# A two-layer trunk on one core: tokens loaded by halves, transposes moved ahead of a last pass, a weight split moved behind the turned h, an add moved to GpSimd

## The chip, the cores and the metric

The kernel runs on one core of one Trainium2 chip. The metric is the device time of one launch in microseconds (us). Engines are named as in the profile: PE (TensorE, matmuls) with PEld (its weight loads), DVE (VectorE), ACT (ScalarE), POOL (GpSimd), SP (SyncE, which here only issues DMAs).

## The reference

Two layers over 256 tokens of width 1024, all in float32. Each layer has a SwiGLU FFN (inner width 2816), a mixer of parallel head groups (SSD, pooling, attention) and a second FFN, each between two RMSNorms:

```python
for l in range(DEPTH):                      # DEPTH = 2
    f = swiglu(rmsnorm(h, ff1_norm_pre[l]), ff1_w_gate[l], ff1_w_up[l], ff1_w_down[l])
    h = h + 0.5 * rmsnorm(f, ff1_norm_post[l])
    m = hybrid_mixer(rmsnorm(h, mix_norm_pre[l]), w_in[l], ..., w_out[l])
    h = h + rmsnorm(m, mix_norm_post[l])
    f = swiglu(rmsnorm(h, ff2_norm_pre[l]), ff2_w_gate[l], ff2_w_up[l], ff2_w_down[l])
    h = h + 0.5 * rmsnorm(f, ff2_norm_post[l])
```

where `swiglu(x, wg, wu, wd) = (silu(x @ wg) * (x @ wu)) @ wd`.

## The kernel before, in words

*Precision.* Every float32 operand of a matmul is cut into two parts, hi (rounded to fp32r) and lo = raw − hi, and a product is hi·hi + lo·hi + hi·lo, three matmuls. For a weight, ACT writes hi (L103) and DVE lo (L104). For activations the same is done by `split_into` (L209 on ACT, L210 on DVE).

*Weights.* The class `Weights` streams all weights in the order of use as units of 1 MB: four slots for raw units (loaded by SP, L78) and five for split ones. `pump` loads the next unit when a slot is free, and otherwise issues the next split. A job can first add a second unit to the first (L102, on DVE). So the time when a unit's load goes out depends on when the work on the unit before it in that slot is finished.

*Tokens.* Two tiles of 128 tokens. Before a sub-layer, `pre_scale` normalises a tile: two squares with sums on ACT (`square_sum`, L226), the sum with eps (L215 on DVE, L218 on ACT), a power −0.5 on POOL (L220), and the scaling on DVE (L252). `pre_turn` then transposes it on PE (L261) and splits the result into xT. For an FFN it also builds the sums and differences of tile quarters that a quad needs (S1 to S4). `post` does the norm behind a sub-layer and adds to h (L234, L243). A tile's work stands beside the other tile's matmuls.

*FFN.* The inner width has 11 blocks of 256. Blocks 0 and 1 come first (`ffn_first`, once per token tile; its matmuls are in `mm_half`, L324). Blocks 4, 7 and 10 are pairs (L305). The others are computed two at a time as quads (`ffn_quad`), by a Strassen-like scheme of seven products (`product`, L435) with the factors X11·g1, S1·T1, S2·T2, S3·T3, X12·g2, X22·T4 and S4·u2. T1 = g1 + u1, T2 = g1 + u2 and T4 = g1 + g2 are formed in the raw buffer of g1; T3 is formed by POOL's accumulating load (L108), which adds u2 to u1 in place. Between the products stand the down matmuls of earlier blocks (`mm_rows`, L341), whose moving operand is the transposed h (`turn`: four PE transposes per half at L410, then the splits into t).

*Mixer.* `first(t)` computes q, k, v of a tile: L313 (`mm_tok`) and L324 (`mm_half`), then the tile's rotary terms.

*Order.* A tile framework takes the instructions in program order and lets its scheduler move those that no `keep_in_program_order` or `issue_after` holds. At the start, SP loads raw0 in one piece, then raw1 in two, x's second tile and the next units; ACT's queue loads x's first tile (L165) and the gains. Constants are loaded after the first quad's `later()`.

Of the kernel before, what the change touches and what calls it, by code (L numbers as in the profile page):

```python
# [14 lines left out]
ALU = mybir.AluOpType  # L15
# [32 lines left out]
class Weights:  # L48
# [23 lines left out]
    def load(self, pieces=1):  # L72
        i = self.loaded
        src, cols = self.units[i]
        t = self.rawp.tile([P, KD * QDT], F32, tag="raw", name=f"raw{i}")
        step = cols // pieces
        for c in range(0, cols, step):
            self.nc.sync.dma_start(t[:, c : c + step], src[:, c : c + step])  # L78
        self.raw[i] = t
        self.loaded += 1  # L80
        self.live += 1
# [32 lines left out]

    def pump(self):
        while True:
            if self.loaded < len(self.units) and self.live < RAW_BUFS:
                self.load()
            elif self.split < len(self.jobs) and self.held < SPLIT_BUFS and self.ready():
                self.split_next()  # L120
            else:
                return
# [16 lines left out]
def hybrid_trunk_kernel(ctx: ExitStack, tc: tile.TileContext, a, out: bass.AP):  # L139
# [24 lines left out]
    h = consts.tile([P, NT, D], F32, name="h")  # L164
    nc.scalar.dma_start(h[:, 0, :], a["x"][:P, :])  # L165
    grow = [buf(tag="n"), buf(tag="n")]
# [45 lines left out]
    def rsqrt_sum(ssq, eps):  # L212

        v, r = tiny(1), tiny(1)
        nc.vector.tensor_scalar(v, ssq[0], eps, None, op0=ALU.add)  # L215
        for s in ssq[1:]:
            w = tiny(1)
            nc.scalar.activation(w, s, AF.Identity, bias=v)  # L218
            v = w
        nc.gpsimd.tensor_tensor(r, v, halfexp, op=ALU.pow)  # L220
        return r

    def square_sum(x, n, gain=1.0):
# [5 lines left out]
    def post(t, f, gain, store=None):  # L229

        fg = [buf(tag="n"), buf(tag="n")]

        def scaled(i):
            nc.vector.tensor_tensor(fg[i], f[i], gains[:, 1, i * 512 : (i + 1) * 512], op=ALU.mult)  # L234

        ssq = [square_sum(f[0], D, gain)]
        scaled(0)
        ssq.append(square_sum(f[1], D, gain))
        r = rsqrt_sum(ssq, EPS / (gain * gain))
        scaled(1)  # L240
# [14 lines left out]
    def pre_turn(t, xn, left=None, late=False):  # L255
# [40 lines left out]
        for i, (name, k, t_) in enumerate((("X11", 0, 0), ("X12", 4, 0), ("X22", 4, 1))):  # L296
# [17 lines left out]

    def mm_half(ps, us, t, pin=False):
# [29 lines left out]
    def plan_ffn(l, n):  # L345
# [15 lines left out]
        for i in range(2, NU):  # L361
# [5 lines left out]
            elif i in QUADS:  # L367
                src = a[f"ff{n}_q"][l, QUADS.index(i)]
                g1, u1, u2 = (W.unit(src[k]) for k in (0, 1, 3))
                p["g1", i] = W.job(g1)  # L370
                p["T1", i] = W.job(g1, (g1, ALU.add, u1), then=(u1, src[3]))
# [24 lines left out]

    def ffn_first(t, p, pin=False):

        ps = [bank(), bank()]
        for i in range(2):  # L400
            mm_half(ps[i], [p["f", i, k] for k in range(2)], t, pin)
        hf = gate(*ps)
        W.pump()
        return hf
# [34 lines left out]
    def ffn_quad(i, p, left, turn, downs):  # L439
# [12 lines left out]
        turn(1)  # L452
        W.pump()
        if "rest" in left:
            left.pop("rest")()
        pb = bank()
# [28 lines left out]
    def ffn(l, n, p, gain, turned, left, next_left, before_next, last, later=None):  # L485

        acc = [None, None]
        hT = {}
        hf = [ffn_first(0, p, pin=later is not None)]
        turned()  # L490
        hf.append(ffn_first(1, p))

# [13 lines left out]
        for i in range(2, NU):  # L506
# [18 lines left out]
            if later:  # L525
                later()
# [10 lines left out]
        if last:  # L537
            post(1, acc[1], gain, before_next)
            return None
        post(1, acc[1], gain)  # L540
        xn1 = before_next(1)
        W.pump()
        return lambda: pre_turn(1, xn1, left=next_left)


    def plan_mix(l):
# [3 lines left out]
        for i, k in enumerate(("B", "C", "x0", "x1", "u")):  # L550
            p[k] = W.plan(a["w_in"][l, i], pieces=2 if i else 4)
        for k in range(2):
# [4 lines left out]

    def mixer(l, p, turned, next_left, before_next):
# [3 lines left out]
        nc.sync.dma_start(row, a["row"][l : l + 1, :].to_broadcast([P, R_ALL]))  # L562

        qk, v, dtr = [], [], small.tile([P, NT, HEADS], F32, tag="dtr", name=f"dtr{l}", bufs=1)

        def first(t):
# [4 lines left out]
            mm_half(pkv, [p["kv", k] for k in range(2)], t)  # L571
            c = buf()
            nc.scalar.activation(c[:, :256], pq[:, :256], AF.Copy)
            nc.vector.tensor_tensor(dtr[:, t, :], pq[:, 256:QDT], row[:, R_DTB : R_DTB + HEADS], op=ALU.add)
            nc.scalar.activation(c[:, 256:], pkv[:, :256], AF.Copy)
            w = buf(n=256)
# [14 lines left out]

        first(0)
        turned()
        first(1)
# [335 lines left out]
        W.done(p["ws1"])  # L930
        post(1, acc[1], 1.0)
        xn1 = before_next(1)
        W.pump()
        return lambda: pre_turn(1, xn1, left=next_left)
# [155 lines left out]
```

## Time and profile before

| | us |
|---|---|
| median of 3 runs | 946.64 (946.31 to 946.86) |
| profiled execution, its own time | 946.24 |
| its span | 944.5 |
| PE busy | 927.3 (98%) |
| PEld busy | 792.5 (84%) |
| DVE busy | 789.1 (84%) |
| ACT busy | 580.8 (61%) |
| POOL busy | 34.9 (4%) |
| DMA | 190.56 MB, mean 202 GB/s |

The clock that PE was granted is full (1.00) in the whole span but its end. The profile is of one execution; the time of that execution is 1.7 us longer than its span. A row of the timeline gives the start, the length, the instruction (out<-in, partitions x elements) and how often it stands in a row; in brackets stands how long the engine idled before it and what released it.

### The profile page before, as it was taken

The numbers are of one execution on the slowest core, as the hardware profiler recorded it, in microseconds if no ns is written. First come the engines' busy times: TensorE is split into PE (matmuls) and PEld (weight loads), VectorE is DVE, ScalarE is ACT, GpSimd is POOL, SyncE is SP. The second block draws the span as 40 slices with busy tenths as digits, with TensorE's granted clock in tenths as the row PEclk, the third lists the DMA queues.
The fourth block names the chain that finished last, engine by engine and source line by source line (L and its number), as shares of the span: only waits on it lengthen the run. The fifth ranks groups of instructions, "written<-read, shape, count | busy, mean of one in ns | idle before, by whom it ended". The sixth has DMA issues, their size and how long they took to land.

```text
span 944.5 us, 13133 instructions
## 1 busy us (share of the span) xinstructions
PE 927.3 (98%) x5058; PEld 792.5 (84%) x5058; DVE 789.1 (84%) x1067; ACT 580.8 (61%) x923; POOL 34.9 (4%) x47
## 2 busy tenths in 40 slices
PE   7999999999999999999999999999999999999997
PEld 4779898989888789898887888898898887989895
DVE  5899898589887998989499989876888799989872
ACT  5666656468737575747467656556694566656651
POOL 1000000010001000000010000000000010000000
PEclk9999999999999999999999999999999999999999
DMA  8757767555343476758463958583833263858531
GB/s 318 224 216 264 263 182 279 213 190 212 134 149 136 135 272 210 284 148 297 173 196 116 352 143 307 146 318 117 275 128 134 90 201 122 329 180 281 177 116 45
DMA packets 28004, 190.56 MB, mean 202 GB/s; under 512 B 3107, under 2 KB 3363, under 8 KB 5925
## 3 DMA queue, kind: packets, MB, share of 16 engines
q1 hardware_dynamic: 25920, 176.34, 51.0%
q0 software_dynamic: 1728, 12.58, 7.3%
q8 instruction: 40, 0.66, 0.3%
q10 hardware_dynamic: 292, 0.79, 0.2%
q14 instruction: 24, 0.19, 0.1%
HBM read 188.65 MB, written 1.05 MB: 201 GB/s over the span
## 4 chain that ended last, share of the span: by engine, by line
PE 85%; DVE 6%; ACT 5%; issue 2%; DMA 2%; POOL 0%; DVEq 0%; POOLq 0%; ACTq 0%
PE acc L341 26%; PE wk L435 22%; PE wk L305 21%; PE wk L324 10%; DVE lo L104 3%; ACT hi L103 3%; PE wk L410 1%; ACT n L226 1%; DMA raw<-in_ff_q 1%; DVE raw L102 1%; PE wk L873 1%; PE wk L261 1%; DMA n<-in_gains 1%; ACT xT L209 1%; POOL s L220 0%
## 5 line engine op out<-in xcount | busy, mean ns | idle before, releaser
L104 DVE TENSOR_TENSOR lo<-raw,hi 128x1024 fp32r<-128x1024 f32 (+2 forms) x440 | 468.1, 1101 | 58.5 <-ACT hi L103 57.5
L103 ACT ACTIVATE hi<-raw 128x1024 fp32r<-128x1024 f32 (+2 forms) x440 | 400.0, 959 | 167.3 <-DVE raw L102 45.4
L341 PE MATMUL acc<-hi,t 128*128 128x512 f32 x832 | 219.9, 394 | 1.8 <-ACT t L209 1.3
L341 PEld LDWEIGHTS acc<-hi,t 128*128 128x128 f32 x832 | 153.1, 188 | 36.4 <-ACT t L209 5.0
L305 PE MATMUL wk<-xT,hi 128*128 128x256 f32 x1088 | 143.5, 284 | 0.0
L305 PEld LDWEIGHTS wk<-xT,hi 128*128 128x128 f32 x1088 | 136.6, 191 | 1.6
L341 PE MATMUL acc<-lo,t 128*128 128x512 f32 x416 | 114.5, 390 | 0.0
L435 PE MATMUL wk<-hi,n 128*128 128x512 f32 x384 | 102.6, 390 | 1.2 <-DVE t L210 1.2
L324 PE MATMUL wk<-hi,xT 128*128 128x512 f32 x384 | 101.1, 396 | 1.8 <-ACT xT L209 1.0
L341 PEld LDWEIGHTS acc<-lo,t 128*128 128x128 f32 x416 | 78.1, 188 | 16.5
L102 DVE TENSOR_TENSOR raw<-raw,raw 128x1024 f32<-128x1024 f32 x72 | 86.1, 1216 | 3.4 <-DMA raw<-in_ff_q 3.4
L324 PEld LDWEIGHTS wk<-hi,xT 128*128 128x128 f32 x384 | 71.1, 189 | 18.9 <-ACT hi L103 2.2
L435 PEld LDWEIGHTS wk<-hi,n 128*128 128x128 f32 x384 | 71.8, 188 | 17.2 <-issue 2.4
L435 PE MATMUL wk<-hi,xT 128*128 128x512 f32 x288 | 77.8, 392 | 0.0
L305 PE MATMUL wk<-xT,lo 128*128 128x256 f32 x544 | 76.8, 283 | 0.0
L305 PEld LDWEIGHTS wk<-xT,lo 128*128 128x128 f32 x544 | 70.3, 192 | 0.0
L435 PEld LDWEIGHTS wk<-hi,xT 128*128 128x128 f32 x288 | 53.6, 188 | 11.5 <-DVE t L466 0.7
L209 ACT ACTIVATE t<-wk 128x256 fp32r<-128x256 f32 x72 | 26.8, 375 | 43.3 <-DVE t L210 22.1
L324 PE MATMUL wk<-lo,xT 128*128 128x512 f32 x192 | 52.6, 393 | 0.1
L435 PE MATMUL wk<-lo,n 128*128 128x512 f32 x192 | 51.5, 389 | 0.0
L234 DVE TENSOR_TENSOR n<-acc,gains 128x512 f32<-128x512 f32 x24 | 16.5, 687 | 35.8 <-ACT n L226 35.8
L324 PEld LDWEIGHTS wk<-lo,xT 128*128 128x128 f32 x192 | 35.9, 188 | 8.6 <-DVE lo L104 1.0
(172 smaller groups left out, 764.8 us busy)
## 6 DMA issues: line engine op xcount, KB each, us to landing
raw<-in_ff_q SPq DMA_DIRECT2D x48, 1024.0 KB, 5.0
raw<-in_ff_d SPq DMA_DIRECT2D x44, 1024.0 KB, 5.0
raw<-in_ff_f SPq DMA_DIRECT2D x16, 1024.0 KB, 6.0
raw<-in_ff_q POOLq DMA_DIRECT2D x12, 1024.0 KB, 8.0
raw<-in_ff_g SPq DMA_DIRECT2D x12, 1024.0 KB, 4.8
raw<-in_ff_u SPq DMA_DIRECT2D x12, 1024.0 KB, 4.9
raw<-in_w_in SPq DMA_DIRECT2D x10, 1024.0 KB, 4.9
raw<-in_w_kvz SPq DMA_DIRECT2D x8, 1024.0 KB, 5.2
```

Of the source, the lines that this page charges most:

```text
L102: nc.vector.tensor_tensor(raw[:, s], self.raw[x][:, s], self.raw[y][:, s], op=op)
L103: self.act = nc.scalar.activation(hi[:, s], raw[:, s], AF.Copy)
L104: nc.vector.tensor_tensor(lo[:, s], raw[:, s], hi[:, s].bitcast(F32), op=ALU.subtract)
L209: split_into.last = nc.scalar.activation(hi, src_f32, AF.Copy)
L226: nc.scalar.activation(junk, x, AF.Square, scale=1.0 / (gain * math.sqrt(n)), accum_out=ssq)
L234: nc.vector.tensor_tensor(fg[i], f[i], gains[:, 1, i * 512 : (i + 1) * 512], op=ALU.mult)
L261: nc.tensor.transpose(ps[:, k * P : (k + 1) * P], xn[i][:, k * P : (k + 1) * P], ident)
L305: nc.tensor.matmul(ps, w[:, k, s], y[:, k, :], start=i == 0 and k == 0, stop=i == 2 and k == KD - 1)
L324: m = nc.tensor.matmul(ps, y[:, k, :], w[:, k, :], start=h == 0 and n == 0, stop=h == 1 and n == len(parts) - 1)
L341: nc.tensor.matmul(acc[b], x[:, j, s], w[:, j, b * 512 : (b + 1) * 512], start=first and j == 0 and i == 0, stop=last and j == 1 and i == 2)
L410: nc.tensor.transpose(ps[:, k * P : (k + 1) * P], hf[:, k * P : (k + 1) * P], ident)
L435: nc.tensor.matmul(ps, x[:, k, :], w[:, k, :], start=first and n == 0, stop=n == len(parts) - 1, skip_group_check=not first)
```

## The change

1. x's first tile is loaded in two halves: the left on SP, ahead of raw0, the right on ACT's queue. raw0 is loaded in two pieces, and two of its four pieces are split ahead of the first xT.
2. `mm_half` takes a function `ahead`, which it calls before the last four matmuls of its second half: the second tile's transposes stand there (in `ffn_first` of the first tile, in the mixer's `first(0)`).
3. In `ffn_quad` the second tile's factors for S3 and S4, and the splits that `pump` issues there (the third factor T3 first), are issued behind the turned h. Those for S1 and S2 (`middle`) move into the second `ffn_first`. The first quad's g1 is split in four pieces instead of two.
4. The eps add moves from DVE to GpSimd (28 instructions); `post` computes both squares ahead of its scalings.
5. Constants, gains, and the first mixer's parameters are loaded behind a later unit, and cast when that unit's split is done; `pump` holds fewer units at some calls, and runs behind a named instruction at others.

The core of the diff:

```diff
@@ def pump
-    def pump(self):
+    def pump(self, most=SPLIT_BUFS):
...
-            elif self.split < len(self.jobs) and self.held < SPLIT_BUFS and self.ready():
+            elif self.split < len(self.jobs) and self.held < most and self.ready():
...
-    nc.scalar.dma_start(h[:, 0, :], a["x"][:P, :])
+    nc.sync.dma_start(h[:, 0, :512], a["x"][:P, :512])
+    nc.scalar.dma_start(h[:, 0, 512:], a["x"][:P, 512:])
...
@@ def rsqrt_sum
-        nc.vector.tensor_scalar(v, ssq[0], eps, None, op0=ALU.add)
+        nc.gpsimd.tensor_scalar(v, ssq[0], eps, None, op0=ALU.add)
...
+    def pump_behind(ins):
+        with tc.issue_after(ins.ins):
+            W.pump()
...
@@ def post
-        ssq = [square_sum(f[0], D, gain)]
+        ssq = [square_sum(f[i], D, gain) for i in range(2)]
+        r = rsqrt_sum(ssq, EPS / (gain * gain))
         scaled(0)
-        ssq.append(square_sum(f[1], D, gain))
-        r = rsqrt_sum(ssq, EPS / (gain * gain))
         scaled(1)
...
@@ def pre_turn
+        def middle():
+            part("S1", s1)
+            nc.vector.tensor_tensor(x11, s1, x11, op=ALU.subtract)
+            part("S2", x11)
...
-        part("S1", s1)
         nc.vector.tensor_tensor(s3, x11, turned[0], op=ALU.subtract)
-        nc.vector.tensor_tensor(x11, s1, x11, op=ALU.subtract)
-        part("S2", x11)
-        left["rest"] = rest
+        left["middle"], left["rest"] = middle, rest
...
@@ def mm_half
+                if ahead and h == 1 and n == 8:
+                    ahead()
...
@@ def ffn_first
-        W.pump()
+        if between:
+            W.split_next()
+            between()
+
+        W.pump(SPLIT_BUFS - t)
...
@@ def ffn_quad
         turn(1)
-        W.pump()
         if "rest" in left:
-            left.pop("rest")()
+            with tc.issue_after(split_into.last.ins):
+                left.pop("rest")()
+                W.pump()
+        else:
+            W.pump()
...
@@ def ffn
-        hf = [ffn_first(0, p, pin=later is not None)]
-        turned()
-        hf.append(ffn_first(1, p))
+        hf = [ffn_first(0, p, later is not None, turned)]
+        middle = left.pop("middle")
+        if later is None:
+            middle()
+        hf.append(ffn_first(1, p, between=middle if later else None))
...
@@ def mixer
-        first(0)
-        turned()
+        first(0, turned)
         first(1)
...
-    W.load()
+    W.load(2)
...
-    W.split_next((0,))
+    W.split_next((0, 1))
...
     def later():
-        more_constants()
-        load_gain(1, 0, 1)
-        load_gain(0, 0, 2)
+        with tc.issue_after(W.dma.ins):
+            more_constants()
+            load_gain(1, 0, 1)
+            load_gain(0, 0, 2)
+            params[0] = load_params(0)
+        with tc.issue_after(W.act.ins):
+            cast_constants()
```

How the instructions stand, before and now, at three places. (Line numbers shift with the change: L209 becomes L214, L210 L215, L324 L336, L261 L269.) First ACT in the first quad of the first FFN. hi6 is the right factor T2, hi7 a down unit, hi8 the factor T3 that the accumulating load completes; t45 and t47 are the turned h. Before:

```order
L103 ACTIVATE hi5_358<-raw4_198 128x1024
L103 ACTIVATE hi6_367<-raw4_198 128x1024
L103 ACTIVATE hi7_375<-raw7_214 128x1024 x2
L209 ACTIVATE t45_391<-wk49_395 128x2x128
L103 ACTIVATE hi8_383<-raw5_200 128x1024
L103 ACTIVATE hi6_367<-raw4_198 128x1024
L103 ACTIVATE hi8_383<-raw5_200 128x1024
L209 ACTIVATE t45_391<-wk54_434 128x2x128
L209 ACTIVATE t47_393<-wk49_395 128x2x128
L209 ACTIVATE t47_393<-wk54_434 128x2x128
```

Now:

```order
L103 ACTIVATE hi6_373<-raw4_200 128x1024
L103 ACTIVATE hi7_381<-raw7_216 128x1024
L214 ACTIVATE t45_389<-wk49_393 128x2x128
L214 ACTIVATE t47_391<-wk49_393 128x2x128
L463 ACTIVATE t51_415<-wk50_402 128x512
L467 ACTIVATE t53_430<-wk52_417 128x512
L214 ACTIVATE t45_389<-wk54_432 128x2x128
L214 ACTIVATE t47_391<-wk54_432 128x2x128
L214 ACTIVATE n55_441<-t34_289 128x512
L103 ACTIVATE hi8_450<-raw5_202 128x1024
```

The splits of hi8 stood between the halves of t45; they now stand behind both t45 and t47, and behind n55, the split of one of the left factors.

Second, PE at the start of the first layer's mixer. The rows L324 (now L336) are `mm_half` of the first tile, with hi43 and hi44 the weights of k and v; L261 (now L269) are the second tile's transposes. Before:

```order
L313 MATMUL wk154_1796<-hi42_1567,xT1_104 128x264 x8
L324 MATMUL wk155_1797<-hi43_1747,xT0_103 128x512 x4
L324 MATMUL wk155_1797<-lo43_1748,xT0_103 128x512 x4
L324 MATMUL wk155_1797<-hi43_1747,xT1_104 128x512 x4
L324 MATMUL wk155_1797<-hi44_1759,xT0_103 128x512 x4
L324 MATMUL wk155_1797<-lo44_1760,xT0_103 128x512 x4
L324 MATMUL wk155_1797<-hi44_1759,xT1_104 128x512 x4
L261 MATMUL wk159_1859<-ident_82,n152_1741 128x128 x4
```

Now:

```order
L323 MATMUL wk154_1794<-hi42_1577,xT1_105 128x264 x8
L336 MATMUL wk155_1795<-hi43_1757,xT0_104 128x512 x4
L336 MATMUL wk155_1795<-lo43_1758,xT0_104 128x512 x4
L336 MATMUL wk155_1795<-hi43_1757,xT1_105 128x512 x4
L336 MATMUL wk155_1795<-hi44_1769,xT0_104 128x512 x4
L336 MATMUL wk155_1795<-lo44_1770,xT0_104 128x512 x4
L269 MATMUL wk157_1843<-ident_83,n152_1751 128x128 x4
L269 MATMUL wk158_1850<-ident_83,n153_1752 128x128 x4
```

The transposes stood behind all 24 matmuls; they now stand ahead of the last four.

Third, DVE in the first quad of the second FFN. raw51 holds g1, and the sum L102 adds g2 from raw55 to it for T4; lo64 belongs to T3, lo65 to g2, and lo66 to the next down unit. Before:

```order
L104 TENSOR_TENSOR lo64_3065<-raw52_2871,hi64_3064 128x1024 x2
L210 TENSOR_TENSOR t331_3073<-wk334_3076,t330_3072 128x2x128
L210 TENSOR_TENSOR t331_3073<-wk339_3115,t330_3072 128x2x128
L286 TENSOR_TENSOR t295_2811<-t295_2811,t294_2809 128x512
L210 TENSOR_TENSOR t333_3075<-wk334_3076,t332_3074 128x2x128
L210 TENSOR_TENSOR t333_3075<-wk339_3115,t332_3074 128x2x128
L102 TENSOR_TENSOR raw51_2617<-raw51_2617,raw55_3062 128x1024
L210 TENSOR_TENSOR n343_3144<-t295_2811,n342_3143 128x512
L104 TENSOR_TENSOR lo65_3125<-raw55_3062,hi65_3124 128x1024 x2
L458 TENSOR_TENSOR t336_3098<-wk344_3147,t336_3098 128x512
L104 TENSOR_TENSOR lo66_3131<-raw56_3070,hi66_3130 128x1024 x2
```

Now:

```order
L215 TENSOR_TENSOR n341_3131<-t319_2978,n340_3130 128x512
L102 TENSOR_TENSOR raw51_2627<-raw51_2627,raw55_3076 128x1024
L215 TENSOR_TENSOR n343_3136<-t295_2821,n342_3135 128x512
L104 TENSOR_TENSOR lo64_3140<-raw52_2881,hi64_3139 128x1024 x2
L104 TENSOR_TENSOR lo65_3148<-raw55_3076,hi65_3147 128x1024 x2
L477 TENSOR_TENSOR t336_3104<-wk344_3161,t336_3104 128x512
L102 TENSOR_TENSOR raw51_2627<-raw51_2627,raw55_3076 128x1024
L478 TENSOR_TENSOR wk337_3106<-wk337_3106,t336_3104 128x512
L484 TENSOR_TENSOR wk349_3224<-wk349_3224,t336_3104 128x512
L485 TENSOR_TENSOR t338_3119<-t338_3119,wk349_3224 128x512
L104 TENSOR_TENSOR lo66_3154<-raw56_3145,hi66_3153 128x1024 x2
```

The T4 sum's first half stood behind lo64, and lo66 one row behind L458, the sum with T2's product. Now that half of the T4 sum and one split of a left factor stand ahead of lo64, and between L477 (the former L458) and lo66 stand four more: the T4 sum's second half, the difference with T2's product (L478), and the two with T3's product (L484, L485).

## Rows read from the trace of the kernel before

**Rows 1.** The page: busy time of PE; groups, with idle time and releaser.
```profile
PE 927.3 (98%) x5058; PEld 792.5 (84%) x5058; DVE 789.1 (84%) x1067; ACT 580.8 (61%) x923; POOL 34.9 (4%) x47
...
L341 PE MATMUL acc<-hi,t 128*128 128x512 f32 x832 | 219.9, 394 | 1.8 <-ACT t L209 1.3
...
L435 PE MATMUL wk<-hi,n 128*128 128x512 f32 x384 | 102.6, 390 | 1.2 <-DVE t L210 1.2
L324 PE MATMUL wk<-hi,xT 128*128 128x512 f32 x384 | 101.1, 396 | 1.8 <-ACT xT L209 1.0
```

**Rows 2.** Chain of waits, first us 50 to 75: start, length, what.
```profile
56.69 5.44 PE wk L435 x24
```

**Rows 3.** Windows from 13 to 180 us: length, busy time by engine, clock, DMA.
```profile
13.00:40.00 27.00, 25.57 (x111) 19.15 (x110) 25.00 (x36) 22.20 (x41) 1.91 (x2) 1.00 0.76 266
40.00:50.00 10.00, 8.72 (x41) 6.88 (x40) 7.00 (x7) 5.14 (x7) 0.00 (x0) 1.00 0.75 198
50.00:180.00 130.00, 129.46 (x717) 112.71 (x716) 115.31 (x126) 81.74 (x103) 1.75 (x2) 1.00 0.71 243
```

**Rows 4.** Timeline of the start: start, length, instruction, idle before and its releaser.
```profile
0.79 0.41 ACTq L165 DMA_DIRECT2D h<-in_x  x1
...
7.30 0.63 ACT L226 ACTIVATE n<-h 128x512 bf16<-128x512 f32 x1 [3.73 <-DMA h<-in_x]
...
7.64 3.75 PE L945 MATMUL acc<-n,n 128*128 128x512 f32 x4 [2.57 <-DMA n<-in_gains]
...
13.88 3.75 ACT L103 ACTIVATE hi<-raw 128x512 fp32r<-128x512 f32 x7
...
28.51 1.20 PE L324 MATMUL wk<-hi,xT 128*128 128x512 f32 x4 [0.23 <-ACT xT L209]
```

**Rows 5.** DMA of the first 25 us, 40 slices.
```profile
GB/s 0 0 39 131 184 446 406 413 465 387 469 423 433 406 367 433 472 419 419 433 420 433 419 380 0 0 0 0 223 170 419 419 419 420 419 433 433 341 406 419
```

**Rows 6.** Timeline, 37 to 54 us, around the turned h.
```profile
37.25 1.03 POOL L108 DMA_DIRECT2D raw<-in_ff_q  x1 [13.70 <-DVE raw L102]
...
45.94 2.95 ACT L103 ACTIVATE hi<-raw 128x1024 fp32r<-128x1024 f32 x3 [4.02 <-DMA raw<-in_ff_q]
...
49.21 0.98 PE L341 MATMUL acc<-hi,t 128*128 128x512 f32 x3 [1.27 <-ACT t L209]
...
51.86 1.88 PE L341 MATMUL acc<-hi,t 128*128 128x512 f32 x7 [0.52 <-DVE t L210]
```

**Rows 7.** Timeline, first layer's mixer start, 199 to 212 us.
```profile
199.36 1.06 ACT L103 ACTIVATE hi<-raw 128x1024 fp32r<-128x1024 f32 x1
...
205.38 1.41 DVE L252 SCALAR_TENSOR_TENSOR n<-h,s,gains 128x512 f32<-128x512 f32 x2 [0.44 <-POOL s L220]
...
208.21 1.25 PE L313 MATMUL wk<-hi,xT 128*128 128x264 f32 x8 [0.36 <-ACT xT L209]
...
211.19 0.55 PEld L313 LDWEIGHTS wk<-hi,xT 128*128 128x128 f32 x4 [0.32 <-DVE xT L210]
```

**Rows 8.** Line L220, whole span, and one instance from the timeline.
```profile
L220 POOL TENSOR_TENSOR s<-s,halfexp x28: 547/870/1437, 9.5 to 939.5; 128x1 f32<-128x1 f32 x28
...
304.25 1.44 POOL L220 TENSOR_TENSOR s<-s,halfexp 128x1 f32<-128x1 f32 x1 [3.42 <-ACT s L218]
```

**Rows 9.** Timeline, 326 to 343 us, first quad of the second FFN.
```profile
326.59 0.33 SPq L78 DMA_DIRECT2D raw<-in_ff_q  x1
...
331.38 1.23 DVE L102 TENSOR_TENSOR raw<-raw,raw 128x1024 f32<-128x1024 f32 x1 [0.63 <-DMA raw<-in_ff_q]
...
336.00 2.35 DVE L104 TENSOR_TENSOR lo<-raw,hi 128x1024 fp32r<-128x1024 f32 x2
...
338.27 0.70 DVE L459 TENSOR_TENSOR wk<-wk,t 128x512 f32<-128x512 f32 x1
...
342.69 1.07 PE L341 MATMUL acc<-lo,t 128*128 128x512 f32 x4
```

**Rows 10.** Timeline, ACT at 110 us.
```profile
109.99 2.01 ACT L103 ACTIVATE hi<-raw 128x1024 fp32r<-128x1024 f32 x2 [2.48 <-issue]
```

More of the change, by code (lines that the diff above doesn't have):

```diff
@@ L77, in load @@
         for c in range(0, cols, step):
-            self.nc.sync.dma_start(t[:, c : c + step], src[:, c : c + step])
+            self.dma = self.nc.sync.dma_start(t[:, c : c + step], src[:, c : c + step])
         self.raw[i] = t
@@ L194, in more_constants, with cast_constants @@
         nc.sync.dma_start(cst, a["consts"])
+    def cast_constants():
         nc.scalar.activation(after_r, after, AF.Copy)
@@ L214, in rsqrt_sum @@
         v, r = tiny(1), tiny(1)
-        nc.vector.tensor_scalar(v, ssq[0], eps, None, op0=ALU.add)
+        nc.gpsimd.tensor_scalar(v, ssq[0], eps, None, op0=ALU.add)
         for s in ssq[1:]:
             w = tiny(1)
-            nc.scalar.activation(w, s, AF.Identity, bias=v)
+            rsqrt_sum.last = nc.scalar.activation(w, s, AF.Identity, bias=v)
             v = w
@@ L313, in mm_tok, with mm_half @@
                 nc.tensor.matmul(ps, x[:, k, s], w[:, k, :], start=i == 0 and k == 0, stop=i == 2 and k == KD - 1)
-    def mm_half(ps, us, t, pin=False):
+    def mm_half(ps, us, t, pin=False, ahead=None):
         for h, u in enumerate(us):
@@ L369, in plan_ffn @@
                 g1, u1, u2 = (W.unit(src[k]) for k in (0, 1, 3))
-                p["g1", i] = W.job(g1)
+                p["g1", i] = W.job(g1, pieces=2 if i > QUADS[0] else 4)
                 p["T1", i] = W.job(g1, (g1, ALU.add, u1), then=(u1, src[3]))
@@ L395, in gate, with ffn_first @@
         return hf
-    def ffn_first(t, p, pin=False):
+    def ffn_first(t, p, pin=False, ahead=None, between=None):
         ps = [bank(), bank()]
         for i in range(2):
-            mm_half(ps[i], [p["f", i, k] for k in range(2)], t, pin)
+            mm_half(ps[i], [p["f", i, k] for k in range(2)], t, pin, ahead if i else None)
         hf = gate(*ps)
-        W.pump()
+        if between:
+            W.split_next()
+            between()
+        W.pump(SPLIT_BUFS - t)
         return hf
@@ L524, in ffn @@
                 before = [i, i + 1]
-            if later:
+            if later and i in PAIRS:
                 later()
@@ L540, in ffn, with turn_second @@
         post(1, acc[1], gain)
+        summed = rsqrt_sum.last
         xn1 = before_next(1)
-        W.pump()
-        return lambda: pre_turn(1, xn1, left=next_left)
+        W.pump(SPLIT_BUFS - 1)
+        def turn_second():
+            pre_turn(1, xn1, left=next_left)
+            pump_behind(split_into.last)
+        if next_left is not None:
+            pump_behind(summed)
+            return lambda: pre_turn(1, xn1, left=next_left)
+        return turn_second
     def plan_mix(l):
@@ L550, in plan_mix @@
         for i, k in enumerate(("B", "C", "x0", "x1", "u")):
-            p[k] = W.plan(a["w_in"][l, i], pieces=2 if i else 4)
+            p[k] = W.plan(a["w_in"][l, i], pieces=2 if i > 1 else 4)
         for k in range(2):
@@ L556, in plan_mix, with load_params @@
         return p
-    def mixer(l, p, turned, next_left, before_next):
+    params = {}
+    def load_params(l):
         vec = small.tile([P, V_ALL], F32, tag="vec", name=f"vec{l}", bufs=1)
@@ L562, in mixer, with first @@
         nc.sync.dma_start(row, a["row"][l : l + 1, :].to_broadcast([P, R_ALL]))
+        return vec, row
+    def mixer(l, p, turned, next_left, before_next):
+        vec, row = params.pop(l) if l in params else load_params(l)
         qk, v, dtr = [], [], small.tile([P, NT, HEADS], F32, tag="dtr", name=f"dtr{l}", bufs=1)
-        def first(t):
+        def first(t, ahead=None):
             pq, pkv = bank(), bank()
@@ L570, in first @@
             last and W.done(p["q"])
-            mm_half(pkv, [p["kv", k] for k in range(2)], t)
             c = buf()
@@ L574, in first @@
             nc.vector.tensor_tensor(dtr[:, t, :], pq[:, 256:QDT], row[:, R_DTB : R_DTB + HEADS], op=ALU.add)
+            mm_half(pkv, [p["kv", k] for k in range(2)], t, ahead=ahead)
             nc.scalar.activation(c[:, 256:], pkv[:, :256], AF.Copy)
@@ L931, in mixer @@
         post(1, acc[1], 1.0)
+        summed = rsqrt_sum.last
         xn1 = before_next(1)
-        W.pump()
+        W.pump(SPLIT_BUFS - 1)
+        pump_behind(summed)
         return lambda: pre_turn(1, xn1, left=next_left)
@@ L947, in hybrid_trunk_kernel @@
     left = {}
-    W.split_next((0,))
+    W.split_next((0, 1))
     keep = pre_turn(0, xn0, left=left, late=True)
     with tc.issue_after(split_into.last.ins):
-        W.split_next((1, 2, 3))
+        W.split_next((2, 3))
         W.load()
```

## The prediction

> **What bounds the kernel now.** I read the head of the page first: PE is busy in 98% of the span [rows 1]. So only what keeps PE from starting, or makes it stop, can change the time. Then the chain of waits: it consists of stretches of matmuls at a fixed pace, 24 of them in 5.44 us (0.227 us each) [rows 2]. The change leaves the number of matmuls as it is, so a gain has to be a PE stall. The groups of the page with their idle time, and then the timeline around each, list the stalls that the diff touches: the start of the program, the wait on the turned h (1.3 of the 1.8 us of the first group shown), the wait on xT (1.0) and three waits on t before a quad's first product (1.2) [rows 1]. Last, the busy time by stretch tells who has room: DVE has 2.0 us left of 27 (13 to 40 us) and 3.0 of 10 (40 to 50), and 14.7 of 130 after that [rows 3]. The reader is to see that PE is first, but DVE only a few us behind it.
>
> **A. The start.** Before, x's first tile (512 KB, one load on ACT's queue, out at 0.79) travels beside raw0's 1 MB. The first square starts at 7.30 after 3.73 us of waiting for x, the matmul that spreads the gains at 7.64 for the gains' row, and the first matmul of the second token tile, behind all the work on the first, at 28.51 [rows 4]. The row of GB/s has slices of 0.625 us: its first ten sum to 1.54 MB at 6.25 us [rows 5], so x arrived with all of raw0, and was seen 1.05 us after that. Now one half of x goes ahead of raw0 on SP, the other on ACT's queue. By the same row 0.50 MB have moved at 3.75 us and 0.75 MB at 4.4. If x shares with nothing, it is seen at 4.8, if the second half shares with raw0, at 5.4. The square of the last half then starts at 4.8 to 5.4 instead of 7.93 (7.30 and one square of 0.63): 2.5 to 3.1 us earlier. The gains' row, queued behind one half, must come as much earlier; I allow 0.3 for it and take −2.4. Further, ACT had one half-unit split ahead of xT and seven behind it (3.75 us, 0.54 each) [rows 4]; it now has two ahead, in time in which it waits anyway, and six behind: −0.54. Sum −2.94, taken as −3.0. Bounds: −1.0 (x seen only 0.5 earlier, and the piece) and −3.5.
> The Trainium skill ("DMA: Bandwidth & Descriptors", Rules for kernel authors) says that two transfers to two halves of the partitions, or spread over issuing engines, share the same 16 DMA engines and bring no bandwidth. The trace agrees as far as it goes: 406 to 469 GB/s while both queues ran, and 419 later with SP's alone [rows 5]. By that rule alone the split would bring nothing, and the sum would be 942.9 (rival 2); but what I count is how many bytes stand ahead of x, not bandwidth.
>
> **B. The turned h in the first quad.** Before, on ACT, the splits of hi8, the third right factor, stand between the two halves of the turned h. They need the unit that POOL's accumulating load completes: out at 37.25, and ACT stands idle for 4.02 us until 45.94. PE therefore waits 1.27 us at 49.21 for ACT's t, and 0.52 at 51.86 for DVE's [rows 6]. Behind each the first matmuls are slow (three in 0.98 where the pace gives 0.68), so together they cost some 2.0 to 2.1. Now the turned h stands ahead of hi8, so both go: −2.0. What is late next: hi8 itself. With A the accumulate goes out near 33 and, if it takes the same 8.6 us, lands near 41.5; PE has the second product and 24 down matmuls (2.7 and 5.4 us) between the turned h and hi8, so hi8 has cover for about 8 us from 42 on. If the cover were gone, its two splits (2 us) would be the price. DVE must follow: A and B take 5.0 us out of a stretch in which it has 2.0 and 3.0 idle [rows 3]. It just fits; each lo that slips costs its slip. Bounds of B: 0 and −2.2.
>
> **C. The mixer's start, twice.** Before, the transposes of the second tile wait at the end of a chain: two squares on ACT with a 1024-wide hi (1.06) between them and the sum, pow on POOL, h, two more squares, DVE's eps add, pow, the scaling (205.38), transposes, xT; PE waits 0.36 for ACT at 208.21 and the weight load 0.32 for DVE at 211.19 [rows 7]; with the slower matmuls behind, some 0.8. Now the two 1024-wide splits are behind, so the sum starts near 199.5, and the scaling near 204.5; and the transposes are emitted ahead of the last four of 24 matmuls, so that xT's split lies beside those (0.9 us). Either would do: I take −0.6 for each of two layers, −1.2, and leave 0.2 each for what the new order costs. Bounds: +0.3 (two adds on POOL of 0.55 each in the chain, against the 0.8) and −0.85 each. The eps add (28 instructions) goes from DVE to POOL. A 128x1 POOL operation lasts 0.55 at the shortest, 0.87 in the median, and 1.44 at 304.25, beside a DVE subtraction [rows 8]. On the paths here it stands behind the first square, and the second square (0.63) still runs beside it, so nothing; without that cover 0.55 to 1.4 a piece, in the chains of C.
> The Trainium skill ("SBUF — State Buffer", Who interferes with whom) goes against this edit: a DVE instruction with two SBUF inputs holds the read port that GpSimd needs. The long pow beside a lo agrees [rows 8]. By it the add could wait one lo, and C would shrink to 0.2 a layer: 941.2, which stays within the forecast's own range.
>
> **D. The first quads of the three later FFNs.** Before, PE waits 1.2 us for t in all ahead of three first products [rows 1], 0.4 each. Now the second product (2.7 us) stands ahead of the down matmuls, and the transposes ahead of the last matmuls of `ffn_first`: that wait, the like for xT at the FFN's start (1.0 in all with the 0.23 of the program's start [rows 1, 4]), and the slow matmuls behind both could go, up to 1.2 in each. But DVE, which works in order, now has the sum for T4 (L102) in front of the splits of the third factor, and that sum waits for the unit of g2: out at 326.59, when the unit before it is cut, seen at 331.38 (4.8 us) [rows 9]. From there to the first lo half of the next down weights DVE has: that sum 1.23, one 0.69, four lo at 1.18, one 0.70, a second sum 1.23, three at 0.70 and the lo 1.18: 11.8 by busy times, 11.0 if each starts 0.07 before the last one's end as in the trace. That is 342.4 to 343.2; PE used this lo at 342.69. So DVE takes back what PE gains: 0. Bounds −1.2 and +1.7 each (the second if the next unit, whose slot comes free only with the third factor's last lo, lands late too).
>
> **E. At nothing.** Constants, gains, vec and row are loaded behind the 20th unit (near 100), and their casts come a few us later: they lie beside ACT idle time such as the 2.48 at 109.99 [rows 10]; without it 2 us. In post both squares come first, which matters in C alone. The tail: the last sum waits for the second square as before, so the add hides. Units cut in four pieces instead of two cost ACT under 0.1 a pair (two of 0.54 against one of 1.06), beside its third of idle time after 50 us [rows 3].
>
> **Sum.** The profiled execution took 946.24, the median of the runs is 946.64, 0.4 above it. 946.24 − 3.0 − 2.0 − 1.2 = 940.0; with the 0.4 the forecast is 940.4 us.
>
> **Rivals.**
> 1. *The first quads gain in full*: the unit of g2 lands sooner, or DVE is not the one PE waits for. For it: PE's stalls there are real [rows 1]; against: DVE's 11.8 us. 940.4 − 3 × 1.2 = 936.8.
> 2. *Tokens no earlier*: the halves still arrive with raw0, since the same DMA engines serve both; A is 0.5. 946.64 − 0.5 − 2.0 − 1.2 = 942.9. Against it: the first 0.5 MB is there by 3.75 us.
> 3. *DVE gives the lead back*: with its room of 5.0 us used up, half of A and B returns as waits for lo before 55 us. 940.4 + 2.5 = 942.9; with C lost too, 944.1, or 944.7 with D at +0.2 each.
> 4. *Slower*: DVE's T4 sum waits for g2. Place: the first quad of three FFNs, on DVE, with every lo of the quad queued behind it and PE waiting for those. If g2 takes 8.6 us to land, as the accumulate did [rows 6], instead of 4.8, the lo is there at 346.2 where PE wants it at 342.69: 3.5 each, 10.5 in all, 950.9. It decides (slower by 0.2% than before) from 2.7 us each, which is a landing of some 7.8 us. For it: the order on DVE is certain; against it: the same kind of load took 4.8 with the same queue.
>
> **Chances.** Forecast 0.50 (own range 938.0 to 942.3), rival 1 0.14, rival 2 0.14, rival 3 0.13, rival 4 0.09. A measurement of this kernel can tell 0.2% (1.9 us) from no change: faster means under 944.7. Forecast, rivals 1 and 2 and half of 3 are faster, 0.84; the other half of 3 (C lost too, and more) is within 0.2%, 0.07; rival 4 is slower, 0.09. The range 936.5 to 945.0 takes in 1 to 3.
>
> **What would show it.** A: the first square near 5 us and tile 1's first matmul near 25.5; if the square is at 6.5 or later, rival 2. B: no PE idle above 0.3 between the first products, and hi8 in place before PE asks for it. C: PE's gap at the L313 matmuls of tile 1 under 0.1. D: the gap between the issue of g2's unit and DVE's T4 sum, and PE's idle at the lo matmuls behind; over 7.8 us the forecast falls. E: no PE gap at the casts. The forecast would be wrong altogether if PE lost its pace of 5.44 us.

## The result, and the profile after

The changed kernel takes 954.48 us (median of 6 runs, 954.26 to 956.18) against 946.34 (946.09 to 946.86): slower, ratio 1.0088, 95% interval 1.0075 to 1.0101. The forecast was 940.4 and faster, with a range that ends at 945.0. The profiled span grew from 944.5 to 952.5.

The page of the changed kernel, the groups that answer to [rows 1] (L341 is now L353, L435 L451, L324 L336):

```profile
PE 929.0 (98%) x5058; PEld 794.4 (83%) x5058; DVE 791.1 (83%) x1051; ACT 582.3 (61%) x935; POOL 41.3 (4%) x75
...
L353 PE MATMUL acc<-hi,t 128*128 128x512 f32 x832 | 218.7, 393 | 0.1
...
L336 PE MATMUL wk<-hi,xT 128*128 128x512 f32 x384 | 103.3, 403 | 11.4 <-ACT t L302 10.9
L451 PE MATMUL wk<-hi,n 128*128 128x512 f32 x384 | 102.2, 390 | 0.0
```

Two of the three waits of before are gone, as forecast (1.8 to 0.1, 1.2 to 0.0). In the third group a new one of 10.9 us stands, on a line that the prediction doesn't name: L302, the copy on ACT in `pre_turn` that reads the second transpose's PSUM bank for S1. The list of PE's waits of the changed kernel (total, times, longest) has it four times, once per FFN:

```profile
PE wk L336 <- ACT t L302: 10.9, 4, 3.0
```

The second FFN's start in the timeline, before (L289 is the later L302) and in the changed kernel:

```profile
308.54 1.03 PE L261 MATMUL wk<-ident,n 128*128 128x128 f32 x8
309.18 1.09 ACT L209 ACTIVATE xT<-wk 128x512 fp32r<-128x512 f32 x2 [4.53 <-PE wk L261]
309.83 1.19 PE L324 MATMUL wk<-hi,xT 128*128 128x512 f32 x4 [0.25 <-ACT xT L209]
...
312.37 0.60 ACT L289 ACTIVATE t<-wk 128x512 f32<-128x512 f32 x1 [2.10 <-DVE xT L210]
```

```profile
307.36 1.03 PE L269 MATMUL wk<-ident,n 128*128 128x128 f32 x8
307.63 2.35 DVE L102 TENSOR_TENSOR raw<-raw,raw 128x1024 f32<-128x1024 f32 x2
307.99 1.09 ACT L214 ACTIVATE xT<-wk 128x512 fp32r<-128x512 f32 x2 [4.38 <-PE wk L269]
...
308.15 1.17 PE L336 MATMUL wk<-hi,xT 128*128 128x512 f32 x4
309.90 1.28 DVE L215 TENSOR_TENSOR xT<-wk,xT 128x512 fp32r<-128x512 f32 x2
...
311.22 0.60 ACT L302 ACTIVATE t<-wk 128x512 f32<-128x512 f32 x1 [2.14 <-DVE xT L215]
...
311.87 1.20 PE L336 MATMUL wk<-hi,xT 128*128 128x512 f32 x4 [2.56 <-ACT t L302]
```

Before, PE started the second tile at 309.83, 2.5 us ahead of that copy. In the changed kernel, the four matmuls at 308.15 are the last of the first tile. The hi half of xT is there at 309.1 (307.99 + 1.09), and the second tile's first four matmuls need no more; yet PE starts at 311.87, 0.05 after L302 ends. L302 writes nothing that they read. What they have in common is PSUM: a pass takes its banks from four (the pool `psum`), the first tile's two outputs hold two, the transposes the other two. The chain to the release is long: here DVE's sum for T1 (L102, 2.35), then the lo half of xT, then L302.

Behind the wait there is a second loss. The windows of the changed kernel (length; busy PE, PEld, DVE, ACT, POOL; granted clock; DMA share and GB/s) right behind the first, second, third and fourth:

```profile
31.00:32.00 1.00, 1.00 (x4) 0.71 (x4) 1.00 (x2) 0.42 (x1) 0.00 (x0) 0.50 0.00 0
...
311.80:313.00 1.20, 1.13 (x5) 0.95 (x6) 1.15 (x2) 0.93 (x3) 0.00 (x0) 1.00 0.90 109
...
496.00:498.00 2.00, 2.00 (x7) 1.51 (x6) 1.97 (x4) 0.00 (x0) 0.00 (x0) 0.51 1.02 213
...
779.00:781.00 2.00, 2.00 (x6) 1.56 (x5) 1.97 (x4) 0.00 (x0) 0.00 (x0) 0.50 0.96 201
```

In three of four the clock falls to 0.50 (1.2 GHz of 2.4) for some 3.5 us once PE works again, and the slow matmuls cost 1.7 us each time.

Matmuls of one shape follow one another at a median spacing. Adding up by how much each matmul starts later than the median spacing behind the shape before it gives PE's stalls by stretch, slow matmuls included (the last column is the first experiment below):

| us lost by PE | before | changed | silu first |
|---|---|---|---|
| 0 to 60 us | 12.7 | 12.4 | 8.8 |
| mixer starts (200 to 220, 660 to 680) | 2.4 | 1.5 | 1.4 |
| later FFNs' starts and first quads (300 to 340, 480 to 520, 760 to 800) | 4.7 | 12.4 | 3.2 |
| rest | 6.3 | 7.4 | 6.6 |
| sum | 26.1 | 33.7 | 20.1 |

33.7 − 26.1 is 7.6 of the 8.0 us by which the span grew.

### The profile page after: what moved, and what is told of

Read it like the earlier page. It is cut to its first block, busy times and chain, and to the rows that moved or that the text cites. A ratio compares the mean times of both kernels' runs of the same rounds, so it can differ in the third digit from the quotient of the medians.

```text
span 952.5 us, 13149 instructions
## 1 busy us (share of the span) xinstructions
PE 929.0 (98%) x5058; PEld 794.4 (83%) x5058; DVE 791.1 (83%) x1051; ACT 582.3 (61%) x935; POOL 41.3 (4%) x75
## 4 chain that ended last, share of the span: by engine, by line
PE 83%; DVE 7%; ACT 4%; issue 2%; DMA 2%; POOL 1%; SPq 0%; POOLq 0%; DVEq 0%; ACTq 0%
PE acc L353 24%; PE wk L451 23%; PE wk L315 21%; PE wk L336 9%; DVE lo L104 3%; ACT hi L103 2%; ACT n L235 1%; PE wk L426 1%; DVE n L260 1%; DMA row<-in_row 1%; DVE xT L215 1%; POOL s L225 1%; PE wk L908 1%; DVE raw L102 1%; DMA raw<-in_ff_f 1%
## 5 line engine op out<-in xcount | busy, mean ns | idle before, releaser
L353 PE MATMUL acc<-hi,t 128*128 128x512 f32 x832 | 218.7, 393 | 0.1
L353 PEld LDWEIGHTS acc<-hi,t 128*128 128x128 f32 x832 | 153.6, 188 | 34.0 <-ACT t L214 3.5
L353 PE MATMUL acc<-lo,t 128*128 128x512 f32 x416 | 115.0, 390 | 0.0
L336 PE MATMUL wk<-hi,xT 128*128 128x512 f32 x384 | 103.3, 403 | 11.4 <-ACT t L302 10.9
L451 PE MATMUL wk<-hi,n 128*128 128x512 f32 x384 | 102.2, 390 | 0.0
L336 PEld LDWEIGHTS wk<-hi,xT 128*128 128x128 f32 x384 | 72.8, 194 | 28.7 <-ACT t L302 12.6
L353 PEld LDWEIGHTS acc<-lo,t 128*128 128x128 f32 x416 | 77.8, 188 | 16.9 <-DVE lo L104 0.6
L102 DVE TENSOR_TENSOR raw<-raw,raw 128x1024 f32<-128x1024 f32 x72 | 86.2, 1219 | 2.7 <-DMA raw<-in_ff_q 2.7
L451 PEld LDWEIGHTS wk<-hi,n 128*128 128x128 f32 x384 | 71.8, 188 | 14.7
L451 PE MATMUL wk<-hi,xT 128*128 128x512 f32 x288 | 77.9, 392 | 0.2 <-DVE t L485 0.2
L451 PEld LDWEIGHTS wk<-hi,xT 128*128 128x128 f32 x288 | 53.4, 188 | 12.1 <-DVE t L485 0.7
L214 ACT ACTIVATE t<-wk 128x256 fp32r<-128x256 f32 x72 | 27.2, 377 | 45.6 <-DVE t L215 31.6
L336 PE MATMUL wk<-lo,xT 128*128 128x512 f32 x192 | 54.7, 406 | 0.1
L451 PE MATMUL wk<-lo,n 128*128 128x512 f32 x192 | 51.4, 389 | 0.0
L336 PEld LDWEIGHTS wk<-lo,xT 128*128 128x128 f32 x192 | 37.3, 195 | 9.0 <-DVE lo L104 0.8
```

The lines of the kernel that those rows point to most:

```text
L102: nc.vector.tensor_tensor(raw[:, s], self.raw[x][:, s], self.raw[y][:, s], op=op)
L214: split_into.last = nc.scalar.activation(hi, src_f32, AF.Copy)
L353: nc.tensor.matmul(acc[b], x[:, j, s], w[:, j, b * 512 : (b + 1) * 512], start=first and j == 0 and i == 0, stop=last and j == 1 and i == 2)
L451: nc.tensor.matmul(ps, x[:, k, :], w[:, k, :], start=first and n == 0, stop=n == len(parts) - 1, skip_group_check=not first)
```

## The experiments

Theory (bank): the second tile's first pass waits for a PSUM bank, since `ahead` puts the reads of the transposes' banks ahead of the gate that frees the first tile's. Rival (late split): it waits for its xT, whose lo half DVE makes late. A time is the median of its runs; the kernel before took 946.1, 945.9 and 946.2 beside the three groups of four. Kernel 1 is the kernel of experiment 1, kernel 7 that of experiment 7. Cuts in a diff are marked by `...`.

**1. The silu of the gate ahead of the second pass**

The silu on ACT is the gate's only read of the first pass's bank; it is made a function of its own and called earlier.

```diff
+    def silu(pg):
...
+            s = silu(ps[0]) if i else None
             mm_half(ps[i], [...], t, pin, ahead if i else None)
-        hf = gate(*ps)
+        hf = gate(*ps, s)
```

> The changed kernel, with the silu of the first tile's gate written ahead of that tile's second pass (it reads a PSUM bank that was complete 5 us before), so that a bank comes free in program order before the transposes' own banks do. Theory (bank): the second tile's first matmul waited for the copy L302 because it was given the bank which that copy reads last; now it gets the gate's bank and needs only the hi half of xT. The four stalls of 2.7 to 3.4 us fall under 0.6 each, and the half clock that followed three of them (about 5 us in all) goes too: 954.5 - 15 = 939.5, between 938 and 942. Rival (late split): the second tile waits for its xT, whose lo half stands on DVE behind two sums of 1.2 us; the bank doesn't matter: 953 to 955.

940.33 (940.02 to 940.53; ratio to before 0.994, 0.9925 to 0.9955), 14.15 under the changed kernel, within the theory's range. Nothing about xT was touched. In its timeline PE runs on for all of the wait, while DVE's sum and L302 stand as late behind the transposes as they did:

```profile
303.41 1.03 PE L269 MATMUL wk<-ident,n 128*128 128x128 f32 x8
303.67 2.35 DVE L102 TENSOR_TENSOR raw<-raw,raw 128x1024 f32<-128x1024 f32 x2
304.04 1.09 ACT L214 ACTIVATE xT<-wk 128x512 fp32r<-128x512 f32 x2 [3.91 <-PE wk L269]
...
304.20 2.07 PE L336 MATMUL wk<-hi,xT 128*128 128x512 f32 x8
305.94 1.28 DVE L215 TENSOR_TENSOR xT<-wk,xT 128x512 fp32r<-128x512 f32 x2
...
307.26 0.60 ACT L302 ACTIVATE t<-wk 128x512 f32<-128x512 f32 x1 [2.13 <-DVE xT L215]
```

The rival is out: the eight matmuls at 304.20 are the first tile's last four and the second's first four, and they start with the hi half of xT alone.

**2. The transposes behind again, in the FFNs**

```diff
-        hf = [ffn_first(0, p, later is not None, turned)]
+        hf = [ffn_first(0, p, later is not None)]
+        turned()
```

> The changed kernel, with the second tile's transposes in the FFNs written behind the first tile's last pass again (in the mixer they stay ahead). Theory (bank): with the gate emitted ahead of the transposes the bank of the gate is free first, the four stalls shrink to the 0.3 to 0.5 us that the kernel before had there, the clock stays full: 940 to 943. Rival (late split): the same late lo half stands there, and the transposes are even later: 954 or more.

940.98 (940.13 to 941.36). The gate is then emitted ahead of the transposes, and the wait for L302 goes. PE's stalls sum to 20.2, against 20.1 in kernel 1, and at the later FFNs to 3.7 against 3.2: in an FFN the new place of the transposes gains little over the old one, even with the wait removed.

**3. The transposes ahead, alone, in the kernel before**

```diff
-        hf = [ffn_first(0, p, pin=later is not None)]
-        turned()
+        hf = [ffn_first(0, p, later is not None, turned)]
...
```

`mm_half` and `ffn_first` take `ahead` as in the change.

> The kernel before, with one part of the change alone: in the FFNs the second tile's transposes are called ahead of the last four matmuls of the first tile's last pass. Theory (bank): this alone makes the new wait, some 2.5 us more than before at each of the four FFNs, and some half clock behind: 946.4 + 10 to 16 = 956 to 962. Rival (late split, or another part of the change together with it): 945 to 948.

958.93 (956.4 to 960.16), 12.8 above before, within the theory's range. No other part of the change is needed for the loss. Its list of PE's waits (L289 is L302 there):

```profile
PE wk L326 <- ACT t L289: 11.2, 4, 2.8
```

**4. DVE's sum held behind the reads of the banks**

```diff
+        if t:
+            with tc.issue_after(pre_turn.read.ins):
...
```

`pre_turn.read` is DVE's last read of the transposes' banks; what the second `ffn_first` issues behind its gate, the sum among it, waits for that read.

> The changed kernel, with DVE's sum for T1 (two instructions of 1.2 us) held behind the splits of xT and the two reads of the transposes' banks. Theory (bank): PE still waits for L302, but L302 is reached earlier where the sum stood in front of the splits (the second to fourth FFN): stalls of about 1.4 instead of 2.7 to 3.1 there, the first FFN's stays near 3; the half clock behind the shorter stalls may go: 954.5 - 4 to 8 = 946 to 951. Rival (late split alone): the stall is gone where the sum was in front, since hi is ready before it: 942 to 946.

945.47 (944.44 to 947.35), 0.5 under the theory's range and inside the rival's, so the time doesn't tell the two apart; the timeline does, since for the rival the wait would be gone. The second FFN in its timeline:

```profile
307.99 1.29 DVE L215 TENSOR_TENSOR xT<-wk,xT 128x512 fp32r<-128x512 f32 x2 [0.92 <-ACT xT L214]
309.31 0.60 ACT L302 ACTIVATE t<-wk 128x512 f32<-128x512 f32 x1 [0.86 <-DVE xT L215]
...
309.96 1.20 PE L336 MATMUL wk<-hi,xT 128*128 128x512 f32 x4 [1.28 <-ACT t L302]
```

The wait shrinks from 2.56 to 1.28 but PE still starts 0.05 behind L302, with xT complete 0.7 before. Behind the shorter waits the clock stays at 1.00; behind the first FFN's, still 2.8, it falls.

The banks themselves stand in the kernels as built, where each buffer has its place. In the changed kernel and in kernels 3 and 4 the second tile's first pass has, in all four FFNs, the bank of the second transpose, which L302 (L289 in kernel 3) reads last; in the kernel before and in kernels 1 and 2 it has the bank of the first tile's first pass, which the silu reads. The wait for that copy stands in the first three and in none of the others.

**5. The sum ahead of raw0's splits at the start**, on kernel 1

```diff
-    W.split_next((0, 1))
+    with tc.issue_after(rsqrt_sum.last.ins):
+        W.split_next((0, 1))
```

> The kernel with the silu first, and at the start ACT's sum for the first tile's norm ahead of the two splits of raw0, which wait for raw0. Theory (queue): x now arrives early, but its norm waits on ACT behind these splits, so only 0.7 of 2.9 us reach the transposes; with the sum first they start near 8.5 instead of 10.3, and the first tile's passes 2 to 2.5 earlier: 937.5 to 938.5. Rival (weights bound the start): the passes wait for raw0's splits anyway, and the time stays within 0.5 of 940.3.

938.7 (938.23 to 940.56), 1.6 under kernel 1. The stalls at 0 to 60 us fall from 8.8 to 7.0; the range given was missed by 0.2. Kernel 1's profile has the half clock from 9.5 to 16.5 us and this one's has none there, so part of the gain may be the clock's.

**6. Tokens whole again**, on kernel 1

```diff
-    nc.sync.dma_start(h[:, 0, :512], ...)
-    nc.scalar.dma_start(h[:, 0, 512:], ...)
+    nc.scalar.dma_start(h[:, 0, :], ...)
...
-    W.load(2)
+    W.load()
...
-    W.split_next((0, 1))
+    W.split_next((0,))
...
-        W.split_next((2, 3))
+        W.split_next((1, 2, 3))
```

> The kernel with the silu first, and x's first tile loaded whole on ACT's queue again, raw0 in one piece, one of its pieces split ahead of xT. Theory: the halves are worth what the second tile's first matmul shows between the kernel before (28.51) and the changed one without its new wait (29.05 - 2.99 = 26.06), 2.4 us: 942.3 to 943. The prediction's term: 3.0, 943.3. Rival (halves bring nothing, the whole gain at the start comes from the order of the splits elsewhere): 940 to 941.

941.22 (940.98 to 941.37), 0.2 above the rival's range: the halves and the second early split are worth 0.9, not 2.4 or 3.0. In the profile both kernels show the half clock between 8.5 and 19.5 us (here the longer), so the halves alone may be worth less than that.

**7. The eps add on DVE again**, on kernel 1

```diff
-        nc.gpsimd.tensor_scalar(v, ssq[0], eps, None, op0=ALU.add)
+        nc.vector.tensor_scalar(v, ssq[0], eps, None, op0=ALU.add)
```

> The kernel with the silu first, and the eps add on DVE again. Prediction's term: nothing (the add lies beside the second square): 940.3 within 0.5. Rival 1 (the add on GpSimd waits for a DVE subtraction and costs in the mixer's start): 939.3 to 939.8. Rival 2 (DVE's queue is what it escapes: there the add stood behind a split of 0.7 to 1.2): 941 to 942.

938.74 (938.56 to 938.87), 1.6 under kernel 1, beyond all three ranges. The first mixer's start in the changed kernel, which answers to [rows 7], then in this one (L220 is now the eps add, L223 ACT's sum, L269 the transposes):

```profile
197.72 1.28 DVE L215 TENSOR_TENSOR xT<-wk,xT 128x512 fp32r<-128x512 f32 x2
...
198.76 0.22 POOL L220 TENSOR_SCALAR s<-s 128x1 f32<-128x1 f32 x1 [5.42 <-ACT n L235]
...
202.64 1.88 DVE L104 TENSOR_TENSOR lo<-raw,hi 128x512 fp32r<-128x512 f32 x3
...
202.97 1.63 POOL L220 TENSOR_SCALAR s<-s 128x1 f32<-128x1 f32 x1 [2.25 <-ACT n L235]
...
204.64 0.30 ACT L223 ACTIVATE s<-s,s 128x1 f32<-128x1 f32 x1 [0.94 <-POOL s L220]
...
206.52 1.29 PE L269 MATMUL wk<-ident,n 128*128 128x128 f32 x8 [0.28 <-DVE n L260]
```

```profile
198.38 0.15 DVE L220 TENSOR_SCALAR s<-s 128x1 f32<-128x1 f32 x1
198.44 1.29 DVE L104 TENSOR_TENSOR lo<-raw,hi 128x512 fp32r<-128x512 f32 x2
...
198.87 0.30 ACT L223 ACTIVATE s<-s,s 128x1 f32<-128x1 f32 x1
...
201.22 1.14 PE L269 MATMUL wk<-ident,n 128*128 128x128 f32 x8
```

On POOL the add takes 0.22 beside a DVE split that reads a PSUM bank and one SBUF tile, and 1.63 beside three subtractions of two SBUF tiles (longer than the longest pow of [rows 8]), and ACT waits 0.94 for it; on DVE it takes 0.15 and the transposes come without a wait. The stalls of the two mixer starts fall from 1.4 to 0.3; the rest of the 1.6 is at the start (7.9 against 8.8), where this kernel keeps the full clock. The Trainium skill ("SBUF — State Buffer", Who interferes with whom) says that a DVE instruction with two SBUF inputs contends with a GpSimd instruction that reads SBUF. The trace agrees, with 1.63 against 0.22.

**8. The weight splits ahead of the turned h again**, on kernel 1

```diff
-        if "rest" in left:
-            with tc.issue_after(split_into.last.ins):
-                left.pop("rest")()
-                W.pump()
...
+        W.pump()
+        if "rest" in left:
+            left.pop("rest")()
```

> The kernel with the silu first, and in the first quad the weight splits (the third factor among them) issued ahead of the turned h again, as in the kernel before. Prediction's step B: the two waits of the kernel before (2.1 us) come back in the first FFN: 942.4, between 942 and 944. Rival (the accumulating load, which now goes out 4 us earlier, has landed by then): 940 to 941.

942.33 (940.39 to 942.55), 2.0 more and within the range of step B, but not where step B had it; one of the four runs took no longer than kernel 1. The accumulate goes out at 34.1 (37.25 in the kernel before, 34.3 in kernel 1) and has landed when ACT comes to hi8, so the first FFN's waits do not return. The loss is in later first quads, above all the last, where a product (L456, in the changed kernel L451) waits for a sum of DVE's:

```profile
803.80 1.16 PE L456 MATMUL wk<-hi,xT 128*128 128x512 f32 x4 [0.84 <-DVE t L487]
```

**9. Kernel 1 with 5 and 7 together**, the scaling too held ahead of raw0's lo splits

> The kernel with the silu first, the eps add on DVE, and at the start the sum and the scaling of the first tile ahead of the two splits of raw0. If the two gains are separate, 1.6 each: 937.1, between 936.6 and 937.8. If both only kept the start from the half clock that the kernel with the silu first showed at 10 to 20 us, they are one gain: 938.4 to 938.8.

937.67 (937.53 to 937.78; ratio to before 0.991, 0.9895 to 0.9925): the best of all, in the range of two separate gains, 8.5 under the kernel before and 16.8 under the changed one. So they aren't one gain, though they overlap: 2.7 of 3.2. Its start, where the sum stands ahead of the split that waits for raw0:

```profile
5.69 0.29 ACT L223 ACTIVATE s<-s,s 128x1 f32<-128x1 f32 x1
...
7.26 1.15 ACT L103 ACTIVATE hi<-raw 128x512 fp32r<-128x512 f32 x2 [1.28 <-DMA raw<-in_ff_f]
8.05 0.60 PE L269 MATMUL wk<-ident,n 128*128 128x128 f32 x4
```

**10. The mixer's transposes behind**, on kernel 7

```diff
-        first(0, turned)
+        first(0)
+        turned()
```

> The kernel with the silu first and the eps add on DVE (938.7), with the second tile's transposes in the mixer behind the whole of the first tile's pass again. Theory (order matters): xT's split is late again for the second tile, some 0.4 to 0.8 in each of two layers: 939.5 to 940.3. Rival (what counted in the mixer's start was the chain of the norm, which is earlier than in the kernel before): 938.4 to 939.0.

940.1 (939.31 to 940.45), 1.4 more: 0.5 of stall returns at each mixer start, and the profile shows some half clock at 10 to 15 us. So in the mixer the new place is worth about what step C took, some of it perhaps the clock's.

**11. Step B alone, in the kernel before**

```diff
@@ def ffn_first
-        W.pump()
+        W.pump(SPLIT_BUFS - t)
...
@@ def ffn_quad
-        W.pump()
         if "rest" in left:
-            left.pop("rest")()
+            with tc.issue_after(split_into.last.ins):
+                left.pop("rest")()
+                W.pump()
...
```

> The kernel before, with the third part of the change alone: the splits of the third factor and of the factors for S3 and S4 behind the turned h, and the smaller limit of pump behind the first blocks that goes with it. Step B of the prediction (the order on ACT makes the two waits): they go, 946.1 - 2.1 = 944.0, if the other first quads don't lose. Rival (the waits came from the accumulating load's late issue, and the order only shifts them to the third factor): 945.5 to 947.

943.35 (943.11 to 943.54), 2.9 under before. The waits at 49.21 and 51.86 [rows 6] are gone, though the accumulate goes out at 36.71, hardly earlier than before. ACT's turned h, no longer behind hi8:

```profile
36.71 1.03 POOL L108 DMA_DIRECT2D raw<-in_ff_q  x1 [13.66 <-DVE raw L102]
...
45.58 1.26 ACT L209 ACTIVATE t<-wk 128x256 fp32r<-128x256 f32 x3 [2.31 <-PE wk L410]
```

**12. Constants early again**, on kernel 7

```diff
-            if later and i in PAIRS:
+            if later:
...
     def later():
-        with tc.issue_after(W.dma.ins):
-            more_constants()
...
+        more_constants()
+        cast_constants()
...
```

> The kernel with the silu first and the eps add on DVE (938.7), with the constants, gains and the mixer's parameters loaded behind the first quad's units and cast there again, as in the kernel before. Prediction's step E (worth nothing, they lie beside idle time): 938.2 to 939.2. Rival (2 MB of loads and three casts between the first quad's units delay its splits): 939.7 to 941.

939.25 (938.64 to 939.8), 0.5 more, with ranges that overlap: nothing that can be told from no change.

## Why the prediction was wrong

*The step that failed* is the one in D that let "the transposes ahead of the last matmuls of `ffn_first`" only take waits away. A moved step was priced by the engine that runs it; what its output holds was not asked. With `ahead` inside the pass, the reads of the transposes' banks come ahead of the gate's in program order, so the next pass is given a bank that a slow chain frees, instead of the gate's, free early. Price: 954.48 − 940.33 = 14.15 us. The waits are 10.9 and the half clock behind three of them is 5.1, neither in the sum nor in a rival; some 2.0 come off, for waits that stand in kernel 1 alone (D below). No row of a trace names a bank; experiments 1 to 4 and the banks of the kernels as built agree on it. In the mixer, where the change also writes the reads that free the first pass's bank ahead of the transposes, the same move made no such wait.

Without that wait the total would have been right (940.33 against 940.4), but by luck and not by its terms. By the table kernel 1 gains 3.9 us at the start, where A and B have 5.0, then 1.0 at the mixers' starts (C: 1.2) and 1.5 at the later FFNs, which D had at nothing:

- **A** (−3.0). x came as forecast; in the changed kernel's start the squares begin at 4.40 instead of 7.30 [rows 4]:

```profile
4.40 0.63 ACT L235 ACTIVATE n<-h 128x512 bf16<-128x512 f32 x1 [0.83 <-DMA h<-in_x]
...
7.27 1.15 ACT L103 ACTIVATE hi<-raw 128x512 fp32r<-128x512 f32 x2 [1.53 <-DMA raw<-in_ff_f]
...
8.33 0.28 ACT L223 ACTIVATE s<-s,s 128x1 f32<-128x1 f32 x1
...
10.49 1.31 PE L269 MATMUL wk<-ident,n 128*128 128x128 f32 x8 [0.74 <-DVE n L260]
```

  But "two ahead, in time in which it waits anyway" was wrong: the two splits wait for raw0 (7.27) and the norm's sum stands behind them (8.33). Of 2.9 us 0.7 reach the transposes (11.18 before). Rival 2's price was nearly right, for another reason. Experiment 5 gets 1.6 back. One reading was off: while both queues ran the row of GB/s also has 387 [rows 5].
- **B** (−2.0) holds in mechanism and was sized too small: alone it gives 2.9 (experiment 11), and by the starts of the matmuls the two waits cost 2.4. Its "three in 0.98 where the pace gives 0.68" sets a length, with the last matmul's whole run in it, against three spacings.
- **C** (−1.2): before, the two starts lost 1.2 each, not 0.8, and 0.9 of these 2.4 us go in the changed kernel. "Either would do" was wrong: the place of the transposes brings 1.0 to 1.4 on top of the earlier chain (experiment 10, with the add on DVE). The add on POOL costs 1.1 (experiment 7), though the prediction had it covered by the second square.
- **D** (0): the waits on t before the first products go in the changed kernel, hidden in its new wait; in kernel 1 three of 0.8 to 1.0 are back, behind DVE's splits, so by the table a gain of 1.5 us is left in all. DVE's T4 sum did not wait for g2 (in the second FFN out at 326.52 and sum at 331.93; no wait for a DMA there or in the other two; [rows 9]), so rival 4 is out: slower came by another way.
- **E** (0) holds within what can be told (experiment 12).

## What to carry to other kernels

When a step moves, ask what its result occupies until when, PSUM banks first: who is given the bank that it would have left, and what stands on each engine ahead of the read that frees it. And on an engine that works in order, a piece put "into waiting time" must not wait for more than what stands behind it.

## What the runs showed of the hardware that was not expected

PE's granted clock falls to 0.50 behind some of its idle stretches of about 3 us, and not behind others of the same length: after three of four waits of 2.6 to 3.0 in the changed kernel, after all four of 2.7 to 2.8 in experiment 3, after none of 1.28 in experiment 4. In the changed kernel it then costs 1.7 us more each time (the slow matmuls in the stalls of the table). At the program's start it fell in some of the kernels too (1, 6, 8, 10 and 12), each seen in one profiled execution, so comparisons of under 1 us there are uncertain. What decides it was not tested.
